# Forming the first shift vector and the first norm's sums on TensorE instead of VectorE and GpSimd

## The chip, the cores and the metric

The kernel runs on one core of one Trainium2 chip. A core has five engines that run side by side and wait for one another through semaphores: TensorE (PE; its weight loads are shown apart as PEld), VectorE (DVE), ScalarE (ACT), GpSimd (POOL) and SyncE (SP), which here only issues DMAs. The metric is the time of one execution in microseconds (us) on the device.

## The reference

Two layers on a residual stream x of 512 positions by 1024 channels, float32: a gated-DeltaNet layer and a differential-attention layer, each followed by an MLP with squared ReLU, and a final norm. Each norm is modulated by a conditioning vector c of 1024 numbers. Only the start is touched by the change:

```python
def rmsnorm(x, g):
    xf = x.astype(jnp.float32)
    y = xf * lax.rsqrt(jnp.mean(xf * xf, axis=-1, keepdims=True) + EPS)
    return (y * g.astype(jnp.float32)).astype(x.dtype)

def modulate(x, g, shift, scale):
    return rmsnorm(x, g) * (1 + scale[:, None, :]) + shift[:, None, :]
...
    cs = jax.nn.silu(c)
...
        mod = cs @ mod_w[l] + mod_b[l]
        sh1, sc1, gt1, sh2, sc2, gt2 = jnp.split(mod, 6, axis=-1)
        if l < N_A_LAYERS:
            h = modulate(x, norm_mix_g[l], sh1, sc1)
            y = gated_deltanet(h, a_w_in[l], ...)
```

So the first h needs the mean of squares over the 1024 channels at each position, and the vectors sh1 and sc1, each a product of silu(c) with a 1024 by 1024 matrix. The first thing done with h is the product with `a_w_in`.

## The kernel before

**Layout.** Activations lie transposed: channels on the 128 partitions, positions along the free dimension. x is eight tiles `x` of 128 channels by 512 positions. A vector over the channels is one column of 128 numbers per channel tile; all the modulation vectors stand in `mod` (128 by 112), where columns 0 to 7 (`SH1`) are the first shift and 8 to 15 (`SC1`) the first scale.

**Modulation columns.** The host hands over `mod_w` transposed, so a column of `mod` is a dot product along the free dimension: `mod_load` (L175 to L179) loads 128 rows of 1024 numbers (0.5 MB) into a tile `mw` through SP's queue, and `mod_dot` (L182) multiplies it on VectorE with `cs`, silu(c) broadcast to all partitions, and sums along the row. A bias is then added (L397), and `mod_gsc` (L209) forms g times (1 + scale) in `gsc`.

**The first norm.** L355 to L375: the eight x tiles are squared, some on VectorE (L366), some on ScalarE (L364), and the squares are added into three accumulators on VectorE and GpSimd (L368, L369). TensorE sums two accumulators over the partitions by taking them as weights against a column of ones (L373): 4 matmuls each, one for each 128 positions, into the bank `psn`. `Norm.finish` (L240 to L253) then forms the mean (L249, VectorE), the power -1/2 (L250, GpSimd), and spreads it over the partitions with four transposes (L252, TensorE) into `rb`.

**The loop over channel tiles.** L390 to L409, two tiles k to a step. For each tile: two modulation columns (shift and scale), their bias, `gsc`, and `modulate` (L259 to L266), which forms `nt` = x times gsc times rb (L262, VectorE), h = nt + shift rounded to the type of the matmul (L264, ScalarE) and the rest that the rounding left (L265, VectorE). `head_weights` (L380) loads the weights of head 0 or 1 (`raw`, three DMAs), and `weights` (L274 to L283) splits them into `wh` (L279, ScalarE) and `wl` (L270, GpSimd here). `three` (L285 to L288) is the product of the two split operands in three matmuls of 128 by 512. Each tile k has three such products for each of the heads 0 and 1, and a further one for the gate weights `wg`, which are all issued in the last step.

After the loop, the projections of heads 0 and 1 go through a convolution (L462 to L471, ScalarE and VectorE), the gates are worked out, and the other six heads follow.

**What sets the order.** The code is written straight out, and a scheduler orders the instructions of each engine ahead of time, by what its timing model takes to be ready, so the order in the trace is not just that of the text. On the chip each engine works in that fixed order. The DMAs that SP issues stand in one queue: x, the masks, then in turn `mw` and `raw` tiles. A load waits until its buffer is free: there are 8 buffers for `mw` in the loop (`MB`), 3 for `raw`, 4 each for `wh` and `wl`, 2 for `nt`.

Of the kernel before, what the change touches and what calls it, by code (L numbers as in the profile page):

```python
# [10 lines left out]
F32 = mybir.dt.float32  # L11
F32R = mybir.dt.float32r
AF = mybir.ActivationFunctionType
ALU = mybir.AluOpType
# [3 lines left out]
P = 128  # L18
D = 1024
KT = D // P  # L20
S = 512
# [9 lines left out]
RAW = 3  # L31
MB = 8
AHEAD = 3
NE = (0, 1, 2, 1, 2, 0, 1, 0)
CV = 9


# [2 lines left out]
C_GMIX = C_KVMODB + 16  # L40
# [43 lines left out]
def trunk_kernel(ctx: ExitStack, tc: tile.TileContext, a, outT):  # L84
    nc = tc.nc
    V, G, A, T = nc.vector, nc.gpsimd, nc.scalar, nc.tensor
# [3 lines left out]
    def nm(s):  # L90
        count[0] += 1
        return f"{s}_{count[0]}"

    def open_pool(name, side="left", bufs=1):
        st = ExitStack()
        p = st.enter_context(tc.tile_pool(name=nm(name), bufs=bufs, side=side, reuse_waits="tile"))
        return p, st

    cp = ctx.enter_context(tc.tile_pool(name="cp", bufs=1))
# [17 lines left out]
    def big(pool, tag, bufs, dt=F32):  # L117
        return pool.tile([P, S], dt, tag=tag, name=nm(tag), bufs=bufs)
# [4 lines left out]
    def bank(tag):  # L123
        return pools["p"].tile([P, S], F32, tag=tag, name=nm("p" + tag), bufs=pools["n"][tag])
# [10 lines left out]
    xs = [None] * KT  # L135
    x_in = a["xT"].rearrange("(k p) s -> p k s", p=P)

    def load_x():
        t = []
        for k in range(KT):  # L140
            xt = big(xp, "x", KT)
            nc.sync.dma_start(xt, x_in[:, k])
            t.append(xt)
        return t

    ones = cp.tile([P, P], F32, name="ones")
    V.memset(ones, 1.0)
    warm = cp.tile([P, 1], F32, name="warm")
    A.activation(warm, ones[:, 0:1], AF.Silu)
    cs = c_pool.tile([P, D], F32, name="cs")  # L150
    nc.scalar.dma_start(cs, a["c"].partition_broadcast(P).rearrange("p a b -> p (a b)"))
    A.activation(cs, cs, AF.Silu)
    xs = load_x()
    cols = cp.tile([P, N_COLS], F32, name="cols")
# [10 lines left out]
    def cc(base, n=1):  # L165
        return cols[:, base:base + n]


    mod = cp.tile([P, 112], F32, name="mod")
    raw_mod = cp.tile([P, 112], F32, name="raw_mod")  # L170
    gsc = cp.tile([P, 40], F32, name="gsc")
# [3 lines left out]
    def mod_load(c, pool=None, bufs=AHEAD + 1):  # L175
        src = a["mod_wT"][c * P:(c + 1) * P, :] if c < 96 else a["kv_mod_wT"][(c - 96) * P:(c - 95) * P, :]
        w = (pool or c_pool).tile([P, D], F32, tag="mw", name=nm("mw"), bufs=bufs)
        nc.sync.dma_start(w, src)
        return w  # L179

    def mod_dot(c, w):
        V.scalar_tensor_tensor(out=w, in0=w, scalar=1.0, in1=cs, op0=ALU.mult, op1=ALU.mult,  # L182
                               accum_out=raw_mod[:, c:c + 1])

    def mod_col(c, pool, bufs):
        mod_dot(c, mod_load(c, pool, bufs))
# [21 lines left out]
    def mod_gsc(j, sc, g, n=8):  # L208
        V.scalar_tensor_tensor(out=gsc[:, j:j + n], in0=mod[:, sc:sc + n], scalar=1.0,  # L209
                               in1=cc(g, n), op0=ALU.add, op1=ALU.mult)  # L210

    SH1, SC1, GT1, SH2, SC2, GT2 = [8 * i for i in range(6)]
# [42 lines left out]
    def h_tiles(pool=None, tag="h", bufs=16):  # L255
        t = [big(pool or hp, tag, bufs, F32R) for _ in range(2 * KT)]
        return t[0::2], t[1::2]

    def modulate(k, x, rb, gs, sh, hi, lo, sl):  # L259
        n = sl.stop - sl.start  # L260
        t = bank("m")[:, 0:n] if "m" in pools["n"] else np_.tile([P, n], F32, tag="nt", name=nm("nt"))
        V.scalar_tensor_tensor(out=t, in0=x[k][:, sl], scalar=gsc[:, gs + k:gs + k + 1], in1=rb,  # L262
                               op0=ALU.mult, op1=ALU.mult)
        A.activation(hi[k][:, sl], t, AF.Identity, bias=mod[:, sh + k:sh + k + 1])  # L264
        V.scalar_tensor_tensor(out=lo[k][:, sl], in0=t, scalar=mod[:, sh + k:sh + k + 1],  # L265
                               in1=hi[k][:, sl].bitcast(F32), op0=ALU.add, op1=ALU.subtract)  # L266
# [7 lines left out]
    def weights(srcs, shape):  # L274
        raw = wp.tile([P] + shape, F32, tag="raw", name=nm("raw"), bufs=RAW)
        for dst, src in srcs(raw):
            nc.sync.dma_start(dst, src)
        wh = wp.tile([P] + shape, F32R, tag="wh", name=nm("wh"))
        A.activation(wh, raw, AF.Copy)  # L279
        wl = wp.tile([P] + shape, F32R, tag="wl", name=nm("wl"))  # L280
        lo_of(wl, raw, wh, lo_on[0])
        mod_next(rate[0])
        return wh, wl  # L283
# [6 lines left out]
    def cols_of(w, c0, n=S, r0=0):  # L290
        v = w.rearrange("(k p) c -> p k c", p=P)
        return lambda k0, nk: (lambda t: [(t, v[:, r0 + k0:r0 + k0 + nk, c0:c0 + n])])
# [61 lines left out]

    m_pool, m_st = open_pool("m", "right")  # L355
    norm = Norm("a")
    acc = [m_pool.tile([P, S], F32, tag="acc", name=nm("acc"), bufs=3) for _ in range(3)]
    for k in range(KT):
        n = NE[k]
        sq = acc[n]  # L360
        if k >= 3:
            sq = m_pool.tile([P, S], F32, tag=f"sq{n}", name=nm("sq"), bufs=2)
        if n:
            A.activation(sq, xs[k], AF.Square)  # L364
        else:
            V.tensor_tensor(out=sq, in0=xs[k], in1=xs[k], op=ALU.mult)  # L366
        if k >= 3:
            (V, V, G)[n].tensor_tensor(out=acc[n], in0=acc[n], in1=sq, op=ALU.add)  # L368
    V.tensor_tensor(out=acc[1], in0=acc[1], in1=acc[0], op=ALU.add)  # L369
    psn = bank("a")  # L370
    for n in (2, 1):
        for t in range(NT):
            T.matmul(psn[:, t:t + 1], lhsT=acc[n][:, t * P:(t + 1) * P], rhs=ones[:, 0:1],  # L373
                     start=n == 2 and t == 0, stop=n == 1, skip_group_check=True)
    rb = norm.finish(FULL, psn)  # L375
    hh, hl = h_tiles()
    w_in = a["a_w_in"]
    v_in = w_in[:, 0:3072].rearrange("(k p) (t c) -> p k t c", p=P, t=3)

    def head_weights(h, k0):  # L380
        return weights(lambda t: [(t[:, :, i, :], v_in[:, k0:k0 + 2, i, h * P:(h + 1) * P]) for i in range(3)],
                       [2, 3, P])
# [7 lines left out]
    for k0 in range(0, KT, 2):  # L390
        ws = []
        for h in range(2):
            k = k0 + h
            mod_col(SH1 + k, m_pool, MB)
            mod_col(SC1 + k, m_pool, MB)
            both = slice(k, k + 9, 8)
            V.tensor_tensor(out=mod[:, both], in0=raw_mod[:, both], in1=cols[:, both], op=ALU.add)  # L397
            mod_gsc(k, SC1 + k, C_GMIX + k, 1)
            modulate(k, xs, rb, 0, SH1, hh, hl, FULL)
            ws.append(head_weights(h, k0))  # L400
        if k0 == 0:
            wg = weights(cols_of(w_in, 4112 - P, P)(0, KT), [KT, P])
        if k0 == KT - 2:

            pg = bank("a")
            for k in range(KT):
                three(pg, wg[0][:, k], wg[1][:, k], hh[k], hl[k], k == 0, k == KT - 1)
        for h in range(2):
            head_pair(ph[h], ws[h], k0)  # L409
# [14 lines left out]
    def gt_(name):  # L424
        return cp.tile([P, NT, H], F32, name=name)

    u, e, w, l, g = gt_("g_u"), gt_("g_e"), gt_("g_w"), gt_("g_l"), gt_("g_g")
# [15 lines left out]
                           op0=ALU.mult, op1=ALU.mult)  # L443
# [326 lines left out]
    def after0(sl, rb):  # L770
        rbs.append(rb)
        for k in range(KT):
# [20 lines left out]
                           op0=ALU.add, op1=ALU.subtract)  # L793
# [155 lines left out]
def host_inputs(inp):  # L949
    f = {k: np.asarray(v) for k, v in inp.items()}  # L950

    def cl(v):
        return v.reshape(-1, P).T

    conv = f["a_conv_w"][0].reshape(4, 24, P).transpose(2, 1, 0).reshape(P, 96)
    packed = np.concatenate(
        [cl(f["mod_b"]), cl(f["kv_mod_b"]), cl(f["norm_mix_g"]), cl(f["norm_mlp_g"]), cl(f["kv_norm_g"]),
         cl(f["final_g"]), conv, cl(f["a_out_norm_g"]), cl(f["b_subln_g"]), cl(f["b_lambda"])], axis=1)
    assert packed.shape == (P, N_COLS)
    r = {  # L960
        "xT": f["x"][0].T,
        "cols": packed,
        "masks": host_masks(),
        "rope": host_rope(),
        "eye": np.tile(np.eye(SUB, dtype=np.float32)[None], (32, 1, 1)),
        "c": f["c"],
        "a_log": f["a_log"],
        "a_dt_bias": f["a_dt_bias"],
        "mod_wT": f["mod_w"].transpose(0, 2, 1).reshape(12288, D),
        "kv_mod_wT": f["kv_mod_w"].T,  # L970
        "a_w_in": f["a_w_in"][0],
        "a_w_out": f["a_w_out"][0],
        "kv_w": f["kv_w"],
        "b_w_q": f["b_w_q"][0],
        "b_w_out": f["b_w_out"][0],
        "mlp_w1": f["mlp_w1"],
        "mlp_w2": f["mlp_w2"],
    }
    return {k: np.ascontiguousarray(v) for k, v in r.items()}
# [16 lines left out]
```

## Time and profile before

| | us |
|---|---|
| median of 3 runs (lowest, highest) | 1396.56 (1394.8, 1398.74) |
| the profiled execution | 1398.15 |
| its span, from the first to the last instruction | 1396.3 |
| TensorE busy in the span | 1315.4 (94%) |
| VectorE busy | 780.9 (56%) |
| ScalarE busy | 510.8 (37%) |
| GpSimd busy | 483.5 (35%) |

A row of the timeline reads: start in us, time in us, engine, line, operation, tile written from tiles read, shapes, and how many such instructions are taken together (x8). What stands in brackets is the time that the engine sat idle just before, and what ended it. A row of the waits reads: engine and line that waited, for whom, total us, times, longest. A row of a view by windows gives, for a stretch of time, the busy time of PE, PEld, DVE, ACT and POOL with the number of instructions, then the clock granted to TensorE (1.00 is full), the share of the DMA engines and GB/s. Matmuls are pipelined: from the start of one to the start of the next is less than the time that a row gives for one.

### The profile page before, as it was taken

To read this page: it belongs to the slowest core of one execution; us is meant where nothing else is said; L and a number is where in the kernel's file an instruction comes from. 1 tells how busy PE (TensorE), PEld (TensorE's weight loads), DVE (VectorE), ACT (ScalarE), POOL (GpSimd) and SP (SyncE) were. 2 spreads that over 40 slices of the span, in tenths; PEclk is the share of its full clock that TensorE was granted. 3 is DMA by queue.
4 is the path that set the end of the run, shared out by engine and by line. 5 is a ranking of instruction groups with operands and counts; after the bars stand their busy time and mean duration, and the time that the engine had idled before them with its cause. 6 is when DMAs were issued, how large, how long until landed. Compare 5 with 4: busy or idle time off the path is not lost. (4 is left out here: it accounts for less than half of the span.)

```text
span 1396.3 us, 19499 instructions
## 1 busy us (share of the span) xinstructions
PE 1315.4 (94%) x7432; PEld 1112.7 (80%) x7432; DVE 780.9 (56%) x1688; ACT 510.8 (37%) x853; POOL 483.5 (35%) x281
## 2 busy tenths in 40 slices
PE   4878998999979999999999999999999999999997
PEld 3666777777758888888889997888798888888897
DVE  6999898899988997001211477777552110031113
ACT  3384354443323433123432344444434331143221
POOL 3324123322013544444444122232235444444441
PEclk9998999999979999999999999999999999999999
DMA  9643123226797786232222232221113323223221
GB/s 313 228 142 76 31 61 90 58 73 188 247 311 272 269 299 228 92 106 91 99 97 91 80 114 87 80 80 65 61 61 106 106 91 103 93 94 103 91 76 61
DMA packets 113214, 174.99 MB, mean 125 GB/s; under 512 B 16384, under 2 KB 56992, under 8 KB 113120
## 3 DMA queue, kind: packets, MB, share of 16 engines
q1 hardware_dynamic: 112416, 172.92, 37.9%
q8 instruction: 58, 0.95, 0.3%
q10 hardware_dynamic: 704, 0.83, 0.2%
q14 instruction: 36, 0.29, 0.1%
HBM read 170.04 MB, written 2.62 MB: 124 GB/s over the span
## 5 line engine op out<-in xcount | busy, mean ns | idle before, releaser
L270 POOL TENSOR_TENSOR wl<-raw,wh 128x1024 fp32r<-128x1024 f32 (+1 forms) x137 | 332.2, 2426 | 414.7 <-ACT wh L279 414.7
L279 ACT ACTIVATE wh<-raw 128x1024 fp32r<-128x1024 f32 (+2 forms) x217 | 215.9, 996 | 500.3 <-PE pj L287 279.8
L286 PE MATMUL pj<-h,wh 128*128 128x512 f32 (+1 forms) x816 | 288.9, 361 | 24.4 <-ACT h L264 6.5
L287 PE MATMUL pj<-h,wh 128*128 128x512 f32 (+1 forms) x816 | 293.1, 360 | 0.7 <-DVE h L265 0.7
L288 PE MATMUL pj<-h,wl 128*128 128x512 f32 (+1 forms) x816 | 291.8, 360 | 0.0
L286 PEld LDWEIGHTS pj<-h,wh 128*128 128x128 f32 x816 | 155.7, 193 | 47.8 <-ACT h L264 8.8
L182 DVE SCALAR_TENSOR_TENSOR mw<-mw,cs 128x1024 f32<-128x1024 f32 x112 | 170.4, 1532 | 6.3 <-DMA mw<-in_mod_wT_dram 4.4
L288 PEld LDWEIGHTS pj<-h,wl 128*128 128x128 f32 x816 | 158.3, 194 | 18.1
L287 PEld LDWEIGHTS pj<-h,wh 128*128 128x128 f32 x816 | 157.9, 194 | 18.5 <-DVE h L265 1.1
L287 PE MATMUL pj<-u,wh 128*128 128x512 f32 (+1 forms) x512 | 172.2, 336 | 0.0
L288 PE MATMUL pj<-u,wl 128*128 128x512 f32 (+1 forms) x512 | 172.2, 336 | 0.0
L286 PE MATMUL pj<-u,wh 128*128 128x512 f32 (+1 forms) x512 | 172.0, 336 | 0.0
L332 DVE SCALAR_TENSOR_TENSOR x<-pj,mod,x 128x256 f32<-128x256 f32 (+1 forms) x53 | 30.5, 585 | 214.8 <-PE pj L288 214.8
L286 PEld LDWEIGHTS pj<-u,wh 128*128 128x128 f32 x512 | 97.2, 190 | 10.1
L288 PEld LDWEIGHTS pj<-u,wl 128*128 128x128 f32 x512 | 97.2, 190 | 10.1
L287 PEld LDWEIGHTS pj<-u,wh 128*128 128x128 f32 x512 | 97.2, 190 | 9.9
L270 DVE TENSOR_TENSOR wl<-raw,wh 128x1024 fp32r<-128x1024 f32 (+2 forms) x80 | 83.0, 1039 | 13.2 <-ACT wh L279 13.0
L751 DVE SCALAR_TENSOR_TENSOR pj<-pj,r 128x512 f32<-128x512 f32 x32 | 21.8, 693 | 81.2 <-ACT r L750 80.9
L751 DVE SCALAR_TENSOR_TENSOR pn<-pn,r 128x512 f32<-128x512 f32 x16 | 11.0, 694 | 92.6 <-ACT r L750 92.6
L286 PE MATMUL pn<-h,wh 128*128 128x512 f32 x128 | 49.8, 389 | 0.0
L287 PE MATMUL pn<-h,wh 128*128 128x512 f32 x128 | 49.8, 389 | 0.0
L288 PE MATMUL pn<-h,wl 128*128 128x512 f32 x128 | 49.8, 389 | 0.0
(295 smaller groups left out, 2373.4 us busy)
## 6 DMA issues: line engine op xcount, KB each, us to landing
raw<-in_mlp_w_dram SPq DMA_DIRECT2D x128, 512.0 KB, 3.6
mw<-in_mod_wT_dram SPq DMA_DIRECT2D x96, 512.0 KB, 5.1
raw<-in_a_w_in_dram SPq DMA_DIRECT2D x96, 128.0 KB, 2.5
mw<-in_kv_mod_wT_dram SPq DMA_DIRECT2D x16, 512.0 KB, 6.4
raw<-in_kv_w_dram SPq DMA_DIRECT2D x16, 512.0 KB, 3.3
x<-in_xT_dram SPq DMA_DIRECT2D x16, 256.0 KB, 6.1
raw<-in_a_w_in_dram SPq DMA_DIRECT2D x16, 256.0 KB, 3.1
raw<-in_a_w_out_dram SPq DMA_DIRECT2D x8, 512.0 KB, 5.0
```

The lines of the kernel that those rows point to most:

```text
L182: V.scalar_tensor_tensor(out=w, in0=w, scalar=1.0, in1=cs, op0=ALU.mult, op1=ALU.mult, accum_out=raw_mod[:, c:c + 1])
L270: (V if n else G).tensor_tensor(out=out, in0=x, in1=hi.bitcast(F32), op=ALU.subtract)
L279: A.activation(wh, raw, AF.Copy)
L286: T.matmul(ps, lhsT=wh, rhs=xh, start=first, stop=False, skip_group_check=skip)
L287: T.matmul(ps, lhsT=wh, rhs=xl, start=False, stop=False, skip_group_check=skip)
L288: T.matmul(ps, lhsT=wl, rhs=xh, start=False, stop=last, skip_group_check=skip)
L332: V.scalar_tensor_tensor(out=x[d][:, sl], in0=ps[j][:, sl], scalar=mod[:, gt + d:gt + d + 1], in1=x[d][:, sl], op0=ALU.mult, op1=ALU.add)
L751: V.scalar_tensor_tensor(out=ps[j], in0=ps[j], scalar=0.0, in1=r, op0=ALU.max, op1=ALU.mult)
```

## The change

Three things change, all ahead of or in the loop over channel tiles.

The squares are no longer added on VectorE and GpSimd: each of the eight square tiles (odd ones formed on VectorE, even ones on ScalarE, in three buffers) is taken as weights against the column of ones, and TensorE accumulates over the tiles in `psn`. A first matmul with zeros starts the accumulation of 16 columns of that bank.

The first shift vector is no longer formed by dots: the host hands over the first 1024 columns of `mod_w[0]` in their natural layout (`mod_sh1`), eight tiles of 0.5 MB are loaded through SP's queue ahead of the loop, and each gives eight matmuls of 128 by 128 weights against one column of `csc`, silu(c) in eight columns. They accumulate in columns 8 to 15 of `psn`, and one add on VectorE puts the bias to all eight columns.

In the loop, the shift's load, its dot and the bias add go. The scale's bias and the 1 are added in one go ahead of the loop (`sc1`), and one instruction forms `gsc`.

```diff
-NE = (0, 1, 2, 1, 2, 0, 1, 0)
...
+    csc = cp.tile([P, KT], F32, name="csc")
+    nc.scalar.dma_start(csc, a["ccol"])
     nc.scalar.dma_start(cs, a["c"].partition_broadcast(P).rearrange("p a b -> p (a b)"))
+    A.activation(csc, csc, AF.Silu)
     A.activation(cs, cs, AF.Silu)
...
-    acc = [m_pool.tile([P, S], F32, tag="acc", name=nm("acc"), bufs=3) for _ in range(3)]
+    zero = cp.tile([P, 16], F32, name="zero")
+    V.memset(zero, 0.0)
+
+    psn = bank("a")
+    T.matmul(psn[:, 0:16], lhsT=ones, rhs=zero, start=True, stop=False, skip_group_check=True)
     for k in range(KT):
-        n = NE[k]
-        sq = acc[n]
-        if k >= 3:
-            sq = m_pool.tile([P, S], F32, tag=f"sq{n}", name=nm("sq"), bufs=2)
-        if n:
+        sq = m_pool.tile([P, S], F32, tag="sq", name=nm("sq"), bufs=3)
+        if k % 2:
+            V.tensor_tensor(out=sq, in0=xs[k], in1=xs[k], op=ALU.mult)
+        else:
             A.activation(sq, xs[k], AF.Square)
-        else:
-            V.tensor_tensor(out=sq, in0=xs[k], in1=xs[k], op=ALU.mult)
-        if k >= 3:
-            (V, V, G)[n].tensor_tensor(out=acc[n], in0=acc[n], in1=sq, op=ALU.add)
-    V.tensor_tensor(out=acc[1], in0=acc[1], in1=acc[0], op=ALU.add)
-    psn = bank("a")
-    for n in (2, 1):
         for t in range(NT):
-            T.matmul(psn[:, t:t + 1], lhsT=acc[n][:, t * P:(t + 1) * P], rhs=ones[:, 0:1],
-                     start=n == 2 and t == 0, stop=n == 1, skip_group_check=True)
+            T.matmul(psn[:, t:t + 1], lhsT=sq[:, t * P:(t + 1) * P], rhs=ones[:, 0:1],
+                     start=False, stop=k == KT - 1, skip_group_check=True)
     rb = norm.finish(FULL, psn)
+    for k in range(KT):
+        w = m_pool.tile([P, D], F32, tag="mw", name=nm("mw"), bufs=MB)
+        nc.sync.dma_start(w, a["mod_sh1"][k * P:(k + 1) * P, :])
+        for c in range(KT):
+            T.matmul(psn[:, 8 + c:9 + c], lhsT=w[:, c * P:(c + 1) * P], rhs=csc[:, k:k + 1],
+                     start=False, stop=k == KT - 1, skip_group_check=True)
+    V.tensor_tensor(out=mod[:, SH1:SH1 + 8], in0=psn[:, 8:16], in1=cols[:, SH1:SH1 + 8], op=ALU.add)
+    sc1 = cp.tile([P, KT], F32, name="sc1")
+    V.tensor_scalar(out=sc1, in0=cols[:, SC1:SC1 + 8], scalar1=1.0, scalar2=None, op0=ALU.add)
...
-            mod_col(SH1 + k, m_pool, MB)
             mod_col(SC1 + k, m_pool, MB)
-            both = slice(k, k + 9, 8)
-            V.tensor_tensor(out=mod[:, both], in0=raw_mod[:, both], in1=cols[:, both], op=ALU.add)
-            mod_gsc(k, SC1 + k, C_GMIX + k, 1)
+            V.scalar_tensor_tensor(out=gsc[:, k:k + 1], in0=raw_mod[:, SC1 + k:SC1 + k + 1], scalar=sc1[:, k:k + 1],
+                                   in1=cc(C_GMIX + k), op0=ALU.add, op1=ALU.mult)
```

More of the change, by code (lines that the diff above doesn't have):

```diff
@@ L966, in host_inputs @@
         "c": f["c"],
+        "ccol": cl(f["c"]),
+        "mod_sh1": f["mod_w"][0][:, 0:D],
         "a_log": f["a_log"],
```

## The prediction

> **What bounds the kernel now.** I read the page first, for the span and for TensorE (PE) and VectorE (DVE) over time.
>
> ```profile
> span 1396.3 us, 19499 instructions
> ...
> PE   4878998999979999999999999999999999999997
> ...
> DVE  6999898899988997001211477777552110031113
> ```
>
> A slice is 34.9 us. PE is at seven tenths or more everywhere but in the first slice, mostly at nine, so only the front can move much; and what moves there moves the end by as much, since PE has little room later to catch up. Next, the timeline of DVE and GpSimd (POOL) in the loop over channel tiles, and one row of the waits of the first 100 us:
>
> ```profile
> 43.13 1.94 POOL L270 TENSOR_TENSOR wl<-raw,wh 128x768 fp32r<-128x768 f32 x1 [3.84 <-ACT wh L279]
> ```
>
> ```profile
> 43.29 2.87 DVE L182 SCALAR_TENSOR_TENSOR mw<-mw,cs 128x1024 f32<-128x1024 f32 x1
> ...
> 46.20 0.16 DVE L397 TENSOR_TENSOR mod<-raw_mod,cols 128x2 f32<-128x2 f32 x1
> 46.39 0.16 DVE L209 SCALAR_TENSOR_TENSOR gsc<-mod,cols 128x1 f32<-128x1 f32 x1
> 46.59 0.75 DVE L262 SCALAR_TENSOR_TENSOR nt<-x,gsc,pa 128x512 f32<-128x512 f32 x1
> 47.25 1.22 DVE L182 SCALAR_TENSOR_TENSOR mw<-mw,cs 128x1024 f32<-128x1024 f32 x1
> ...
> 48.40 0.75 DVE L265 SCALAR_TENSOR_TENSOR h<-nt,mod,h 128x512 fp32r<-128x512 f32 x1
> 49.06 2.87 DVE L182 SCALAR_TENSOR_TENSOR mw<-mw,cs 128x1024 f32<-128x1024 f32 x1
> ```
>
> ```profile
> ACT h L264 <- DVE nt L262: 35.4, 8, 6.3
> ```
>
> DVE is full: 49.06 - 43.29 = 5.77 us a tile. Two of its instructions are dots of L182, one of 1.22 us and one of 2.87 us, the second ending 1.1 us after the POOL subtraction beside it. ScalarE (ACT), which forms h, waits 35.4 us for DVE in these eight tiles. So **DVE bounds the loop**. Then PE's first and last matmul of the loop, with its rates, from PE's timeline:
>
> ```profile
> 22.16 1.65 PE L286 MATMUL pj<-h,wh 128*128 128x512 f32 x3 [1.59 <-ACT h L264]
> 23.61 0.63 PE L287 MATMUL pj<-h,wh 128*128 128x512 f32 x1
> 24.04 0.63 PE L288 MATMUL pj<-h,wl 128*128 128x512 f32 x1
> ...
> 27.45 0.45 PE L287 MATMUL pi<-h,wh 128*128 128x512 f32 x1
> ...
> 29.71 0.39 PE L287 MATMUL pj<-h,wh 128*128 128x512 f32 x1
> 29.94 0.39 PE L288 MATMUL pj<-h,wl 128*128 128x512 f32 x1
> ```
>
> ```profile
> 71.57 0.39 PE L288 MATMUL pr<-h,wl 128*128 128x512 f32 x1
> ```
>
> The loop issues 8 tiles x (2 heads x 3 + 1 gate tile) x 3 = 168 such matmuls. From start to start they take 0.43 us at first and 0.227 us from 27.45 us on. Dense, they need 168 x 0.227 = 38.1 us; they take 71.8 - 22.16 = 49.6 us. So 11.5 us are idle or slow PE: that is what a shorter DVE chain could win at most, if PE began no later.
>
> **The change: what leaves DVE.** Per tile one dot (1.22), the bias add of L397 (0.16), and before the loop the adds of squares. The second dot, nt, lo and gsc stay: 1.22 + 0.16 + 0.75 + 0.75 = 2.9 us a tile, some 1.65 more (2.87 - 1.22) if it meets POOL: 4.5 us, against 38.1 / 8 = 4.8 us of dense PE. PE then sets the pace of the loop. Stalls of 0 to 3 us may stay, since 4.5 and 4.8 are close; dots and nt of the first tiles, done ahead of the first h, speak for 0, which I take.
>
> **What PE gets.** A matmul of two f32 operands is two instructions, each with a weight load (L373 and L246 below: 4 calls are x8, 2 calls x4). New on PE ahead of the loop: squares, 8 tiles x 4 x 2 = 64 instructions (now 16); shift, 8 x 8 x 2 = 128 (now 0); the 4 transposes of L252 stay. All 8 shift columns come out of one add that reads the finished sums, so **no h can be formed before the 128th instruction** - today the first h needs two dots only. This is the step that decides. The price of one, by the nearest rows (PE and its loads, PEld):
>
> ```profile
> 15.32 1.86 PE L373 MATMUL pa<-ones,acc 128*128 128x1 f32 x8 [1.91 <-DVE acc L369]
> 19.45 1.11 PE L252 MATMUL pa<-mask,rs 128*128 128x128 f32 x4 [2.27 <-POOL rs L250]
> ```
>
> ```profile
> 430.38 0.54 PEld L246 LDWEIGHTS pn<-ones,acc 128*128 128x128 f32 x4
> 430.84 0.19 PEld L288 LDWEIGHTS pj<-h,wl 128*128 128x128 f32 x1
> ```
>
> ```profile
> 156.09 0.97 PEld L598 LDWEIGHTS pi<-z,um 128*128 128x128 f32 x8
> ```
>
> ```profile
> 117.57 0.80 PE L539 MATMUL pa<-cv 128*128 128x128 f32 x2 [1.17 <-ACT ex L519]
> 118.16 0.63 PE L540 MATMUL pa<-cv,cv 128*128 128x128 f32 x2
> 118.59 0.64 PE L539 MATMUL pa<-cv 128*128 128x128 f32 x2
> ```
>
> L373 has one of 0.352 us, so its eight start (1.86 - 0.352) / 7 = 0.215 us apart; the pairs at 118.16 and 118.59 give 0.43 / 2 = 0.215. On a fast PE, L598 gives (0.97 - 0.19) / 7 = 0.111 and L246 (430.84 - 430.38) / 4 = 0.115. **Bounds: 0.111 and 0.215 us**, and which one holds is a question of the clock:
>
> ```profile
> 38.00:40.00 2.00, 2.00 (x6) 1.58 (x5) 2.00 (x1) 0.00 (x0) 1.30 (x1) 0.50 1.11 330
> ```
>
> Here the granted clock (third number from the end) is 0.50, after PE had idled, and six matmuls start in 2 us. So 0.43 us means half clock. The start of the trace runs at that pace, though the page shows 1.0 there; I go by the spacing. From 22.16 to 27.45 PE issued dense 512-column matmuls, and after 5.3 us the clock was full. Will a stream that loads 128 columns of weights and moves one column do the same? No row has such a stream beyond eight instructions. The eight of L373 ran at half clock throughout, and the only streams seen to lift it move 128 to 512 columns an instruction. I take **half clock, 0.215 us, to the end of the shift**; the other end goes to the rivals.
>
> **When PE starts and what else could bind**, from the timelines and one window:
>
> ```profile
> 0.73 0.41 ACTq L151 DMA_DIRECT2D cs<-in_c_dram  x1
> ...
> 5.55 1.06 ACT L152 ACTIVATE cs<-cs 128x1024 f32<-128x1024 f32 x1 [2.88 <-DMA cs<-in_c_dram]
> ...
> 10.30 0.63 ACT L364 ACTIVATE sq<-x 128x512 f32<-128x512 f32 x1 [0.15 <-DMA x<-in_xT_dram]
> ...
> 21.39 0.72 ACT L264 ACTIVATE h<-nt,mod 128x512 fp32r<-128x512 f32 x1 [3.00 <-DVE nt L262]
> ```
>
> ```profile
> 0.00:25.00 25.00, 7.68 (x27) 6.51 (x28) 13.95 (x24) 9.15 (x13) 7.98 (x10) 1.00 0.92 311
> ```
>
> The small additions (zeros and their matmul, sc1, the eight-column c with its Silu) lie before the first square, where PE and DVE are idle; the new DMA stands ahead of that of cs on ACT's queue and may delay its Silu by one issue, 0.41 us, which I leave in the rounding. The first square follows that Silu (5.55 + 1.06 + 0.63, about 7.3 us); the seventh x is there by 10.30, faster than PE at 0.215 takes squares (1.7 us a tile). DMA: x 2.10, cs 0.52, cols 0.13, mask 0.39 and the eight shift loads 4.19 MB make 7.3 MB, at 311 GB/s 23.6 us, so PE is later than DMA in every case. The eight loads fill the eight buffers of "mw", so the first scale load, and behind it on SP's queue the first head weights, wait until PE has used the first shift tile; they have some 20 us until they are needed, and are hidden. The wait adds nothing on POOL's queue. The power of L250 and the transposes of L252 can lie between shift matmuls; if PE waits for them instead, it costs 1 to 3 us (upper bound).
>
> **Sum.** Squares 64 x 0.215 = 13.8, from 7.3 to 21.1; transposes 0.9, to 22.0; shift 128 x 0.215 = 27.5, to 49.5. Read-out, add and hops some 0.5, h 0.72: first loop matmul at **50.7 us** (now 22.16). The loop then is dense: 38.1 us, and 2.5 us for another 5.3 us at half clock (half of them lost): end at 91.3 us, now 71.8: **+19.5 us**. Given back behind it: DVE comes to the convolutions free.
>
> ```profile
> 66.40 0.96 DVE L270 TENSOR_TENSOR wl<-raw,wh 128x768 fp32r<-128x768 f32 x1
> 67.88 0.96 DVE L270 TENSOR_TENSOR wl<-raw,wh 128x768 fp32r<-128x768 f32 x1 [0.53 <-ACT wh L279]
> 68.76 1.22 DVE L182 SCALAR_TENSOR_TENSOR mw<-mw,cs 128x1024 f32<-128x1024 f32 x1
> 69.90 2.72 DVE L468 SCALAR_TENSOR_TENSOR cv<-pj,cols,cv 128x511 f32<-128x511 f32 x4
> ```
>
> It starts them at 69.90, 1.9 us before PE's last loop matmul ends, behind three instructions that could be done earlier; with head 0 finished one head (18 x 0.227 = 4.1 us) before that end it can start 2.2 us earlier. Bounds 0 to 4; I take 2.2. Net **+17 us**: 1398.15 (the profiled execution, span 1396.3 and 1.85 around it) becomes 1415. The median of the runs is 1.6 lower, so I say **1414**. Own range: 0 to 4 given back, 0 to 3 lost in waits, and part of the stream at full clock at the end: 1408 to 1420.
>
> **Rivals.**
> *A. The one-column stream lifts the clock* (not slower). It is decided by one thing, whether weight loads with one moving column count as activity; for it speaks that PE would be continuously occupied for 40 us, against it the rows above. As in the first loop matmuls, 5.3 us at half clock (25 instructions, to 12.6), then 39 x 0.111 to 16.9, transposes 0.5, shift 14.2, to 31.6; first loop matmul 32.8, dense to 70.9: 0.9 earlier than now, 2.2 more from DVE: -3, or 1393.5, with stalls up to 1397. The point between gain and loss is a price of about 0.13 us. By the Trainium skill, "TensorE: Matmul & The Clock Gate", Part 1, the clock doubles after about 3.4 us of sustained PE activity; by that rule this rival holds, since the stream is sustained. The same page's Part 4 says that transposes do not count as busy in the same way, so activity there is not just occupancy; no run here shows which it is for one moving column.
> *B. The same, and DVE's free start is worth more* (4 us, or the clock lifts at once, saving up to 2.5): about 1390.5. The loop's 11.5 us of slack on PE is the most there is, and the 192 new or kept one-column instructions at 0.111 take 21 us from 7.3 us on, so no more than this.
> *C. Half clock, and PE also waits* for the power and the transposes, and for scale loads that were issued late: 3 to 5 us more, 1418 to 1421. DVE's and SP's free time speaks against it.
>
> **How the numbers follow.** Forecast 0.54, A 0.30, B 0.08, C 0.08. A measurement of this kernel tells about 0.3%, or 4.2 us, from no change. Faster by more: B and a little of A, 0.10. Within: most of A, 0.26. Slower: forecast, C and a little of A, 0.64. The range, 1391 to 1420, takes in A and the forecast's own range, leaving half of B and of C.
>
> **What would show it.** In the new trace: starts of the shift matmuls 0.215 or 0.111 us apart; the first loop matmul at about 51 or 33 us; the loop then 38 to 41 us long with little idle; the convolutions beginning about 4 us before the loop's last matmul ends. I am wrong if the stream runs fast, if the first h is formed before the stream's end, or if the later stages catch up what the front lost.

## The result, and the profile after

| | before | after |
|---|---|---|
| median, us (lowest, highest) | 1397.65 (1394.8, 1398.91), 4 runs | 1415.74 (1413.95, 1419.5), 4 runs |
| ratio to before | | 1.0128, 95% interval 1.0104 to 1.0151 |
| profiled execution, span | 1396.3 | 1412.2 |
| first matmul of the loop | 22.16 | 54.49 |
| end of the loop's last matmul | 71.8 | 101.25 |

The change makes the kernel 1.3% slower. The page of the kernel after, for the same rows as before:

```profile
span 1412.2 us, 19826 instructions
...
PE   7898899999989999999999999999999999999997
...
DVE  0499999998998999601211277777652110021113
```

PE is now busier in the first slice than before (7 in place of 4), and DVE has nearly nothing to do there (0 in place of 6). A busy share says nothing of the pace; PE's timeline from the first square to the loop shows it:

```profile
8.29 1.86 PE L371 MATMUL pa<-ones,sq 128*128 128x1 f32 x8 [6.60 <-ACT sq L369]
10.72 12.11 PE L371 MATMUL pa<-ones,sq 128*128 128x1 f32 x56 [0.57 <-DVE sq L367]
23.09 13.81 PE L378 MATMUL pa<-csc,mw 128*128 128x1 f32 x64 [0.25 <-DVE rs L251]
36.76 1.09 PE L254 MATMUL pa<-mask,rs 128*128 128x128 f32 x4
37.65 13.65 PE L378 MATMUL pa<-csc,mw 128*128 128x1 f32 x64
54.49 0.79 PE L288 MATMUL pj<-h,wh 128*128 128x512 f32 x1 [3.19 <-ACT h L266]
...
55.87 0.63 PE L290 MATMUL pj<-h,wl 128*128 128x512 f32 x1
56.30 0.63 PE L288 MATMUL pj<-h,wh 128*128 128x512 f32 x1
```

```profile
8.29:51.30 43.01, 42.19 (x196) 41.93 (x196) 3.12 (x9) 4.06 (x6) 3.11 (x3) 1.00 0.62 210
```

The 56 instructions from 10.72 on come 12.11 / 56 = 0.216 us apart, the first 64 of the shift 13.81 / 64 = 0.216 and the last 64 13.65 / 64 = 0.213: the pace that the prediction took for half clock, from the first to the last, through 43 us of a stream without a gap of a microsecond. The granted clock of the profile does not show it. It reads 1.00 for this whole stretch, as it did at the start of the kernel before, so the clock is read from the spacing. The loop's first matmuls bear that out: they too start 0.43 us apart (55.87 and 56.30), not 0.227. L288 waits 3.19 us for its first h. DVE's timeline says why it waits so long:

```profile
22.87 0.16 DVE L251 TENSOR_SCALAR rs<-pa 128x4 f32<-128x4 f32 x1 [4.37 <-PE pa L371]
51.34 0.17 DVE L380 TENSOR_TENSOR mod<-pa,cols 128x8 f32<-128x8 f32 x1 [28.31 <-PE pa L378]
51.42 1.22 DVE L184 SCALAR_TENSOR_TENSOR mw<-mw,cs 128x1024 f32<-128x1024 f32 x1
...
52.94 0.75 DVE L264 SCALAR_TENSOR_TENSOR nt<-x,gsc,pa 128x512 f32<-128x512 f32 x1
...
56.40 1.65 DVE L402 SCALAR_TENSOR_TENSOR gsc<-raw_mod,sc,cols 128x1 f32<-128x1 f32 x1
58.09 0.75 DVE L264 SCALAR_TENSOR_TENSOR nt<-x,gsc,pa 128x512 f32<-128x512 f32 x1
```

In DVE's fixed order the add L380, which needs the last shift sum, stands ahead of the first scale dot (L184). DVE idles 28.31 us, and only then does the dots, one tile after another: from the first nt to the second it takes 58.09 - 52.94 = 5.15 us. So in the first half of the loop DVE is the bound again, and the loop lasts 101.25 - 54.49 = 46.8 us.

The loop ends 29.4 us later than before, yet the span is only 15.9 us longer: 13.5 us came back behind the loop. The next view, by windows, sets the stretch from the loop's end to the first ReLU of the MLP (the heads, the gates and the first projection) side by side. The first line of a pair is all engines (PE, PEld, DVE, ACT, POOL), the second only the dots and the reads of their sums, two rows to a dot. Before:

```profile
71.80:467.90 396.10, 355.60 (x2332) 293.91 (x2332) 358.66 (x940) 167.88 (x283) 100.88 (x71) 0.95 0.46 143
```

```profile
71.80:467.90 396.10, 82.25 (x127) 0.95 0.46 143
```

After:

```profile
101.25:479.60 378.35, 347.07 (x2332) 289.06 (x2332) 341.84 (x915) 161.58 (x279) 94.38 (x71) 0.97 0.43 137
```

```profile
101.25:479.60 378.35, 71.63 (x109) 0.97 0.43 137
```

PE's 2332 instructions are the same, but DVE has nine dots less in the stretch (18 rows) and is busy 16.8 us less, and the stretch is 17.8 us shorter. These are dots for later layers; in the kernel after, three of the nine stand ahead of the stretch, in the loop, and six behind it. PE's same instructions also took 8.5 us less (355.6 and 347.1), at a granted clock of 0.97 in place of 0.95. Whether PE ran faster because it waited less for DVE, or for a reason of its own, is not shown. From that ReLU to the end of the trace the span is 4.2 us longer than before (932.6 against 928.4).

### The profile page after: what moved, and what is told of

Read it like the earlier page. It is cut to its first block, busy times and chain, and to the rows that moved or that the text cites. A ratio compares the mean times of both kernels' runs of the same rounds, so it can differ in the third digit from the quotient of the medians.

```text
span 1412.2 us, 19826 instructions
## 1 busy us (share of the span) xinstructions
PE 1344.5 (95%) x7610; PEld 1146.2 (81%) x7610; DVE 778.8 (55%) x1663; ACT 506.2 (36%) x851; POOL 479.0 (34%) x280
## 5 line engine op out<-in xcount | busy, mean ns | idle before, releaser
L272 POOL TENSOR_TENSOR wl<-raw,wh 128x1024 fp32r<-128x1024 f32 (+1 forms) x137 | 339.1, 2478 | 430.9 <-ACT wh L281 430.8
L288 PE MATMUL pj<-h,wh 128*128 128x512 f32 (+1 forms) x816 | 291.1, 361 | 17.8 <-ACT h L266 9.0
L290 PE MATMUL pj<-h,wl 128*128 128x512 f32 (+1 forms) x816 | 288.4, 356 | 0.3 <-DVE wl L272 0.3
L288 PEld LDWEIGHTS pj<-h,wh 128*128 128x128 f32 x816 | 155.6, 192 | 39.9 <-ACT h L266 10.8
L288 PE MATMUL pj<-u,wh 128*128 128x512 f32 (+1 forms) x512 | 172.0, 336 | 0.0
L184 DVE SCALAR_TENSOR_TENSOR mw<-mw,cs 128x1024 f32<-128x1024 f32 x104 | 162.2, 1576 | 10.0 <-DMA mw<-in_mod_wT_dram 9.1
L290 PEld LDWEIGHTS pj<-u,wl 128*128 128x128 f32 x512 | 97.2, 190 | 12.5 <-POOL wl L272 2.4
L288 PEld LDWEIGHTS pj<-u,wh 128*128 128x128 f32 x512 | 97.2, 190 | 9.9
L288 PE MATMUL pn<-h,wh 128*128 128x512 f32 x128 | 49.8, 389 | 0.0
```

The costliest lines, as they stand in the source:

```text
L272: (V if n else G).tensor_tensor(out=out, in0=x, in1=hi.bitcast(F32), op=ALU.subtract)
L288: T.matmul(ps, lhsT=wh, rhs=xh, start=first, stop=False, skip_group_check=skip)
L290: T.matmul(ps, lhsT=wl, rhs=xh, start=False, stop=last, skip_group_check=skip)
```

## The experiments

Times are medians; "before" was run beside each group and came to 1397.7 (beside the kernel after), 1399.3, 1399.5 and 1398.7, so the ratios compare better than the medians. Two numbers locate what a kernel does: the first loop matmul, and the stretch from the loop's end to the first ReLU.

| kernel | median | ratio to before (95%) | first loop matmul | loop | stretch | DVE busy in it |
|---|---|---|---|---|---|---|
| before | | 1 | 22.2 | 49.6 | 396.1 | 358.7 |
| after | 1415.7 | 1.0128 (1.0104 to 1.0151) | 54.5 | 46.8 | 378.4 | 341.8 |
| 128 moving columns | 1403.2 | 1.0017 (1.0002 to 1.0031) | 40.0 | 45.1 | 384.7 | 345.1 |
| scale dots first | 1428.4 | 1.0195 (1.0169 to 1.0221) | 57.9 | 40.7 | 394.8 | 362.3 |
| both | 1424.2 | 1.0166 (1.0142 to 1.0190) | 44.9 | 43.4 | 401.6 | 364.8 |
| shift only | 1414.4 | 1.0097 (1.0064 to 1.0131) | 49.3 | 48.3 | 384.8 | 344.6 |
| squares only | 1396.2 | 0.9977 (0.9967 to 0.9987) | 32.4 | 48.5 | 384.1 | 349.6 |
| before, late dots held | 1402.4 | 1.0027 (1.0013 to 1.0041) | 22.1 | 49.7 | 382.1 | 336.2 |
| after, late dots held | 1423.4 | 1.0172 (1.0151 to 1.0193) | 54.5 | 46.1 | 374.7 | 330.8 |
| 128 columns, late dots held | 1410.3 | 1.0077 (1.0060 to 1.0093) | 41.3 | 45.5 | 376.3 | 330.9 |
| after, more dots in the heads | 1428.4 | 1.0202 (1.0181 to 1.0223) | 54.5 | 48.3 | 392.1 | 354.3 |
| squares only, 128 columns | 1392.4 | 0.9956 (0.9940 to 0.9972) | 26.0 | 47.0 | 385.0 | 350.1 |
| 32 moving columns (one run) | 1423.4 | | 54.1 | 48.3 | 382.7 | 344.6 |

**128 moving columns in the shift stream.** The prediction's open question was whether the stream runs at half clock because it moves one column at a time.

```diff
+    pw = [bank("i") for _ in range(2)]
...
-            T.matmul(psn[:, 8 + c:9 + c], lhsT=w[:, c * P:(c + 1) * P], rhs=csc[:, k:k + 1],
-                     start=False, stop=k == KT - 1, skip_group_check=True)
+            T.matmul(pw[c // 4][:, c % 4 * P:c % 4 * P + 128], lhsT=w[:, c * P:(c + 1) * P],
+                     rhs=csc[:, k:k + 1].to_broadcast([P, 128]), start=k == 0 and c % 4 == 0, stop=k == KT - 1,
+                     skip_group_check=True)
```

> The shift matmuls move 128 equal columns in place of one, into two banks of their own; nothing else. Theory (the clock is lifted by moved columns, not by weight loads): the shift instructions start 0.215 us apart for one or two of the 3.4 us steps seen in the clock, then 0.111; the stream ends 10 to 12 us earlier (about 40 in place of 51.3 us), the first loop matmul comes at about 43, and the loop begins at full clock, 2.5 us more: 1415.7 - 13 = about 1402. Rival (0.215 us is simply what an f32 weight load costs there, or the clock only follows from the loop's type of matmul): spacing stays 0.215, first loop matmul 54.5, 1415 +- 3.

PE's timeline of this kernel:

```profile
22.70 7.57 PE L379 MATMUL pi<-csc,mw 128*128 128x128 f32 x52
30.11 0.60 PE L254 MATMUL pa<-mask,rs 128*128 128x128 f32 x4
30.54 8.65 PE L379 MATMUL pi<-csc,mw 128*128 128x128 f32 x76
39.97 0.96 PE L288 MATMUL pj<-h,wh 128*128 128x512 f32 x3 [0.78 <-ACT h L266]
```

The same weights, the same number of instructions, 128 times the columns, and the stream is faster: the last 76 take 8.65 us, 0.114 each. The first 52 take 7.57: start by start, the first 15 of them, to 25.9 us, still ran at half clock, 3.2 us. That time is not fixed. In "both" the same stream, begun at 28.01, came to the faster pace after 4.8 us, and in "128 columns, late dots held" after 5.9 us, so that its first 52 took longer:

```profile
22.69 8.86 PE L379 MATMUL pi<-csc,mw 128*128 128x128 f32 x52
```

The kernel gains 12.5 us over the one after by the medians, 1.1% or some 15 us by the ratios, and stands level with the one before but for 0.2%. The theory holds; the rival (0.215 is the price of an f32 weight load) falls. The level total does not mean that the front costs nothing now: the first loop matmul comes 17.8 us later than in the kernel before and the loop ends 13.3 us later (85.1 and 71.8), and 11.4 us of that come back in the stretch (384.7 and 396.1).

**32 moving columns**, the same edit with 32 in place of 128.

> As the variant with 128 moving columns, but 32 columns. If what lifts the clock is the share of time in which columns are moved (32 of the 128 that fill the time of a weight load, a quarter), spacing stays 0.215 and the first loop matmul comes at about 54, 1415. If any matmul beyond one column counts, it is as with 128: 0.111, about 40, 1403.

```profile
22.68 13.84 PE L379 MATMUL pi<-csc,mw 128*128 128x32 f32 x64
...
37.22 13.70 PE L379 MATMUL pi<-csc,mw 128*128 128x32 f32 x64
54.11 0.79 PE L288 MATMUL pj<-h,wh 128*128 128x512 f32 x1 [3.19 <-ACT h L266]
```

13.70 / 64 = 0.214 us: no lift. So it is not any column beyond the first that counts; the boundary lies between 32 and 128 columns to a weight load. This run also has the two banks of its own and the same adds as the one with 128, so these are not what lifted the clock there. (That this single run took 1423 us and not 1415 lies behind its first loop matmul: loop, stretch and the rest are 1.5, 4.3 and some 4 us longer than in the kernel after. Why was not followed up.)

**Scale dots first.** The eight scale loads and their dots stand ahead of the shift in the text, so that L380 no longer holds them.

```diff
     rb = norm.finish(FULL, psn)
+    for k in range(KT):
+        mod_col(SC1 + k, m_pool, MB)
...
-            mod_col(SC1 + k, m_pool, MB)
```

> The eight scale loads and their dots stand ahead of the shift loads, so that VectorE is not held by the add that waits for the shift sums. Theory (the add L380 blocks the dots behind it in VectorE's fixed order; this costs the first h some 2 us and the loop some 6 us): first loop matmul about 52.5 in place of 54.5, loop 40 to 41 us in place of 46.8, 1415.7 - 8 = about 1408. Rival (the loop's length comes from PE's and POOL's own work): loop stays above 45, 1414 +- 2.

PE's timeline of this kernel, its DMA queue, and the two lines by windows:

```profile
28.13 27.44 PE L380 MATMUL pa<-csc,mw 128*128 128x1 f32 x128 [1.83 <-DMA mw<-in_mod_sh_dram]
57.92 0.80 PE L288 MATMUL pj<-h,wh 128*128 128x512 f32 x1 [2.36 <-ACT wh L281]
```

```profile
24.29 10.67 SPq L378 DMA_DIRECT2D mw<-in_mod_sh_dram  x8
```

```profile
98.66:493.50 394.84, 350.84 (x2332) 290.32 (x2332) 362.27 (x949) 169.41 (x286) 95.09 (x71) 0.96 0.48 150
```

```profile
98.66:493.50 394.84, 85.68 (x133) 0.96 0.48 150
```

The loop did shrink, to 40.7 us as expected, so the held dots were what stretched it. But the shift loads now wait for the buffers of the dots (issued from 24.29 on, 9.69 before), the first loop matmul comes later still, and the scheduler's order has 12 dots more in the stretch behind the loop (133 rows against 109), which grew by 16.5 us. The expected total, 1408, was missed by 20 us. The edit was right about its own place and wrong about the whole.

**Both edits.**

> Both edits. If the half clock and the blocked dots are the whole cost, first loop matmul at about 41, loop 38 to 40, its end at about 80 in place of 101: 1415.7 - 21 = about 1395, level with the kernel before (1397). If what is gained in the front is given back in the later heads, as some 10 us of the loss were, about 1403.

First loop matmul 44.9 and loop 43.4, some 4 us worse each than expected; the stretch, with 135 rows of dots, is 401.6 us. The total of 1424 met neither number. What it adds is one more point: many dots in the stretch, a long stretch.

**Shift only**: squares added on VectorE and GpSimd as before, the rest as after.

```diff
-        for t in range(NT):
-            T.matmul(psn[:, t:t + 1], lhsT=sq[:, t * P:(t + 1) * P], rhs=ones[:, 0:1], ...
+        if k >= 3:
+            (V, V, G)[n].tensor_tensor(out=acc[n], in0=acc[n], in1=sq, op=ALU.add)
```

> The squares are added on VectorE and GpSimd as before; only the shift comes from TensorE. Theory (the stream is PE-bound at 0.215 us): 48 instructions less, the stream can begin when the first shift tiles land (15 us) and ends about 44 in place of 51.3; first loop matmul about 48, and with the loop as it is now 1415.7 - 7 = about 1409. Rival (the squares were hidden behind the loads anyway): 1414 +- 2.

The front did as expected: first loop matmul 49.3, 5.2 us earlier than after. The total, 1414.4, stands where the rival put it, though its interval also holds the theory's 1409 (1.0069 of the kernel before). In the traces, of the front's gain the loop took 1.5, and the stretch, with the same 109 rows of dots, was 6.4 us longer than after's (384.8 against 378.4). In "128 moving columns" too it is 384.7 with 109 rows. So a spread of some 6 us in this stretch is not explained by dots.

**Squares only**: squares on TensorE, shift by dots as before.

```diff
-    V.tensor_tensor(out=mod[:, SH1:SH1 + 8], in0=psn[:, 8:16], in1=cols[:, SH1:SH1 + 8], op=ALU.add)
...
+            mod_col(SH1 + k, m_pool, MB)
             mod_col(SC1 + k, m_pool, MB)
```

> Only the squares are summed by TensorE; the shift comes from dots as before. Theory (one-column instructions cost 0.215 us at half clock, and the first h waits for them): the 64 instructions run from 8.3 to 22.8, the first nt comes at about 26 in place of 20.6, the first loop matmul at about 27.5 (22.16 before), and the dots that VectorE does meanwhile shorten the loop by 2 to 3: 1399 + 2 to 4 = 1401 to 1403. Rival (the adds of squares on VectorE were the dearer way): 1396 or less.

```profile
25.01 1.12 PE L254 MATMUL pa<-mask,rs 128*128 128x128 f32 x4 [2.26 <-POOL rs L252]
32.42 1.65 PE L288 MATMUL pj<-h,wh 128*128 128x512 f32 x3 [6.29 <-ACT h L266]
```

Its front is worse than expected (32.4 in place of 27.5, the loop ends 9.1 us later than before), and its time is better: 0.23% below before, where a loss was expected. The stretch again gives back more than the front loses, 12 us, with 121 rows of dots in place of 127. So this half of the change costs nothing, and the shift is what costs.

**Late dots held back.** Is it the dots? In the kernels before and after and in the one with 128 columns, the dots whose text stands behind the heads cannot be drawn forward, since `cs` is rewritten in place (plus zero) once the last head is done.

```diff
     rate[0] = 1
+    zc = cp.tile([P, 1], F32, name="zc")
+    V.tensor_scalar(out=zc, in0=oT[H - 1][:, 0:1], scalar1=0.0, scalar2=None, op0=ALU.mult)
+    A.activation(cs, cs, AF.Identity, bias=zc)
     g_st.close()
```

> The kernel before, with the dots that its text has behind the heads (modulation columns of later layers) held back until the last head is done, by an in-place copy of cs that waits for that head (adding zero to it). In its VectorE order 60 - 36 = 24 dots leave the heads' last stretch. Theory (the stretch of the heads is bound by VectorE, and the dots that the fixed order pulls into it cost their 1.24 us each until PE binds; this is where the kernel after got back part of its loss): the stretch from the last head's diagonal blocks to its end, 93.7 us with PE busy 83.6, shrinks by 6 to 10 us: 1399 - 8 = about 1391. Rival (the order's PE waits made the difference, not the dots): 1399 +- 2.

> The same edit on the kernel after: 47 - 29 = 18 dots leave the stretch, which was 89.5 us with PE busy 80.9. Theory: 4 to 8 us, about 1409, so that it stands about 18 us behind the edited kernel before. If the shorter stretch of the kernel after came from anything else than dots, 1415.

> The same edit on the variant with 128 moving columns (1403): theory about 1396 to 1397, below the kernel before (1399) but not below the kernel before with the same edit; rival 1403.

In the kernel before the stretch shrank by 14.0 us (396.1 to 382.1) with 20 dots less in it; after's by 3.7 and the wide one's by 8.4, with 12 less each. So dots in this stretch do cost time, but not at a fixed price. None of the expected totals came: all three kernels became slower, by 3 to 8 us, since the dots come due right behind. From the waits of PE between the first ReLU and the attention, and the windows of that time, of the kernel before with held dots and then of the kernel before itself:

```profile
PE pj L286 <- DVE x L332: 11.7, 1, 11.7
```

```profile
453.80:874.90 421.10, 406.09 (x2104) 348.75 (x2104) 222.75 (x317) 137.13 (x195) 169.91 (x70) 0.98 0.47 156
```

```profile
467.90:873.90 406.00, 402.19 (x2105) 346.18 (x2104) 180.61 (x273) 137.04 (x195) 162.71 (x70) 1.00 0.40 135
```

PE once waits 11.7 us for the residual add L332, and the 14 us won are lost there (421.1 against 406.0). The two other kernels have the same wait, of 8.7 us (after) and 11.4 us (128 columns). Where the stretch gains from dots that leave it, they must not be in the way later; the nine that the change itself moved were not, the 12 and 20 held back here were.

**More dots in the heads**: the kernel after, with later modulation columns taken at a higher rate in the heads and gates.

```diff
-    rate[0] = 0.5
+    rate[0] = 0.7
     heads = []
...
-    rate[0] = 0.5
+    rate[0] = 0.7
     for i in range(0, H, 2):
```

> The kernel after, with the rate of later modulation columns raised from 0.5 to 0.7 per weight tile in the heads and gates: in VectorE's fixed order 10 more dots stand between the loop and the end of the heads (45 in place of 35; the kernel before has 43), and 10 fewer later; front and total work are the same. Theory (the heads are bound by VectorE, and the kernel after got back its loss there because its order holds fewer dots in that stretch): from the loop's end to the first ReLU of the MLP 378 us become about 390, some 2 to 4 us come back in the MLP, in total 1415.7 + 8 = about 1424. Rival (the stretch is shorter because of something else, as the clock's steps): 1416 +- 2.

```profile
102.80:494.90 392.10, 352.65 (x2333) 290.95 (x2332) 354.34 (x935) 161.41 (x281) 98.26 (x70) 0.97 0.46 144
```

```profile
102.80:494.90 392.10, 81.98 (x127) 0.97 0.46 144
```

With as many rows of dots as the kernel before (127), the stretch is 392.1 us (390 expected), 13.7 us longer than after's and near before's 396.1. The total rises by 12.7 (1424 was expected): the loop took 1.5 us more, and nothing came back behind the stretch, which the expectation had at 2 to 4 us (932.6 us, as in the kernel after). In direction this is the mirror image of what the change did. The size is less sure: 13.7 us for nine dots here, 3.7 for twelve above, and kernels with the same 109 rows differ by 6.3.

**Squares only, 128 columns of ones**, the two findings put together:

```diff
-            T.matmul(psn[:, t:t + 1], lhsT=sq[:, t * P:(t + 1) * P], rhs=ones[:, 0:1],
-                     start=False, stop=k == KT - 1, skip_group_check=True)
-    rb = norm.finish(FULL, psn)
+            T.matmul(psn[:, t * P:(t + 1) * P], lhsT=sq[:, t * P:(t + 1) * P], rhs=ones,
+                     start=k == 0 and t == 0, stop=k == KT - 1, skip_group_check=True)
+    rb = norm.finish(FULL, psn.rearrange("p (t f) -> p t f", f=P)[:, :, 0])
```

> Squares on TensorE against 128 columns of ones in place of one, the shift by dots as before. Theory (moved columns lift the clock): the 64 instructions end at about 18 in place of 22.8, the first loop matmul comes 4 to 5 us earlier than with one column (32.4), 1396.2 - 3 = about 1393, below both kernels. Rival (first h bound by its two dots and the loads, or the gain is lost in the heads): 1396 +- 1.

```profile
8.43 6.76 PE L367 MATMUL pa<-ones,sq 128*128 128x128 f32 x40 [8.43 <-ACT sq L365]
15.83 3.27 PE L367 MATMUL pa<-ones,sq 128*128 128x128 f32 x24 [0.63 <-DVE sq L363]
...
25.96 1.65 PE L288 MATMUL pj<-h,wh 128*128 128x512 f32 x3 [1.59 <-ACT h L266]
```

The squares' sums are done at 19.1 in place of 22.8, the first loop matmul comes 6.4 us earlier than with one column, and the time is 1392.4 us, 0.44% below before: the fastest kernel of the study.

## Why the prediction was right, point by point

- **"No h can be formed before the 128th instruction", at 0.215 us each**: right, and it decides the case. Squares and shift took until 51.3 us, forecast 49.5. The variant with 128 columns shows that the price is the clock's: at 0.11 us the same stream costs 12.5 us less, and the kernel loses next to nothing (1.0017). That is near rival A's time, but not by rival A's path. A wanted one moved column to lift the clock, which it did not, and had the first loop matmul at 32.8; here it comes at 40.0, and 11.4 us come back in the stretch far behind. The Trainium skill ("TensorE: Matmul & The Clock Gate", Part 1) has the clock double after about 3.4 us of sustained PE activity. With 128 moving columns the traces roughly agree (3.2, 4.8 and 5.9 us in three kernels); with 1 column in 43 us and with 32 in 28 us they do not, so a stream can occupy PE and still not be activity in that sense.
- **"The dots and nt of the first tiles, done ahead of the first h"**: wrong. L380 stood ahead of them in DVE's order. Of the 3.8 us by which the first loop matmul was later than forecast (54.5 against 50.7) the stream itself was 1.8 late, 1.0 of it because it began at 8.3 and not at 7.3; the other 2.0 are the dot, gsc and nt that had to wait behind L380, for which the forecast had no time there. The loop was 6.2 us longer than forecast (46.8 against 40.6), and "scale dots first" shows it at 40.7 without the blocked dots.
- **"Given back: 2.2 us, bounds 0 to 4"**: mis-sized. 13.5 us came back, and the prediction's first step, that "what moves there moves the end by as much", failed with it: of 29.4 us at the loop's end 15.9 reached the end. The earlier convolutions, as forecast, are part of it: head 0's diagonal blocks leave for memory 28.2 us behind the loop's end in place of 31.7, 3.5 us. Dots are another part: nine of them were no longer placed in that stretch, and with nine put back the stretch is 13.7 us longer. How much of the 17.8 us is theirs stays open, since the price of a dot differed so much between the runs and PE's granted clock changed too. That the order of a far stage would change with the front was in no term of the sum.
- **The total**: +17 forecast, +18.1 in the medians, +15.9 in the spans. The first term, the late start, carries it; the rest was wrong by +10 us (3.8 at the first loop matmul, 6.2 in the loop) and by -11 us (behind the loop), which cancel. The closeness of the number is luck, its sign and cause are not.
- **The rivals**: B (faster) falls with A. C (waits for the power and the transposes) did not come: L254 stands among the shift matmuls without idle time before it.

Still open: why the scheduler places fewer dots in the stretch in the kernel after, and what makes the stretch 378 us in one kernel and 385 in others with the same 109 rows of dots. In part it is PE's own pace: its 2332 instructions are busy 347.1 us at a granted clock of 0.97 in the kernel after, 349.8 at 0.96 in the one with 128 columns.

## What to carry to other kernels

A matrix-vector product with the matrix as weights occupied TensorE fully here and yet left its clock at half; price it by the slow row, or give it 128 equal moving columns, which cost nothing here beside the weight loads and brought 12.5 us. Before one sum is put ahead of eight tiles that used to start one by one, ask what the first tile now waits for, and what stands behind that wait in each engine's fixed order. And where a scheduler orders by a model, an edit at the front can move work between stages far behind: compare the instruction counts by stage of both traces before a gain or a loss is put down to the edit itself.

## What the runs showed of the hardware that was not expected

The number of moved columns to a weight load decided whether the clock rose: 1 and 32 did not lift it (0.213 to 0.216 us an instruction, over 43 and 28 us), 128 did, after 3.2 to 5.9 us (0.114). And in the loop of the kernel after a DVE instruction of one column, L402 at 56.40, took 1.65 us (0.22 us at 52.68) while a POOL subtraction ran:

```profile
55.25 2.79 POOL L272 TENSOR_TENSOR wl<-raw,wh 128x768 fp32r<-128x768 f32 x1 [20.91 <-ACT wh L281]
```

It ended just as that one did, at 58.04. In five more of the eight tiles L402 took 1.65 to 2.23 us, each time ending with the subtraction beside it; in the two tiles in which none was running when it began it took 0.22 and 0.21. In "squares only" two other small instructions met two subtractions in the same way, before the first nt, which is part of why that kernel's front was later than expected:

```profile
25.27 1.64 DVE L395 TENSOR_TENSOR mod<-raw_mod,cols 128x2 f32<-128x2 f32 x1
26.94 1.72 DVE L211 SCALAR_TENSOR_TENSOR gsc<-mod,cols 128x1 f32<-128x1 f32 x1
```

```profile
24.93 3.72 POOL L272 TENSOR_TENSOR wl<-raw,wh 128x768 fp32r<-128x768 f32 x2
```

The 1.65 us that the prediction put on a dot fell on such small instructions, so it is the meeting with POOL and not the size that is paid for.
